# Low parts of split weights by an accumulating DMA instead of a VectorE subtraction

## The chip, the cores and the metric

The kernel runs on one core of a Trainium2 chip. The metric is the device time of one execution in microseconds (us), as the median over runs. The engines are TensorE (PE for its matmuls, PEld for its weight loads), VectorE (DVE), ScalarE (ACT), GpSimd (POOL) and SyncE (SP), which issues all transfers of the kernel before the change.

## The reference

Two layers of a trunk with 512 latent tokens and 256 context tokens, width 1024, in float32. In each layer one wide projection `h @ w_in` (1024 by 7456) feeds three branches: grouped-query attention, a chunked bidirectional gated linear attention (GLA) and a gated mixing MLP (SGU). Each branch is gated and projected, the three are merged under sigmoid gates, projected by `w_out`, and normalised:

```python
h = x * (1 + scale) + shift
parts = split(h @ w_in)
m = sig(m_a) * (y_attn @ w_br_attn) + sig(m_g) * (y_gla @ w_br_gla) + sig(m_s) * (y_sgu @ w_br_sgu)
x_new = layer_norm(ALPHA * x + gate * (m @ w_out))
```

Layer 0 computes all 768 tokens in its output, layer 1 only the 512 latent ones.

## The kernel before

**Split products.** TensorE's fast 32-bit format keeps fewer bits than float32. So each operand of a large product is held as a high part (the value rounded to that format) and a low part (the value minus the high part). A product is three matmuls: high by high, low by high, high by low. `mm3` issues them for one block of 128 rows of the contraction.

**Weights.** `wgroup(src, nkb, c0, n)` brings a group of `nkb` blocks of 128 rows and `n` columns (mostly 8 or 4 blocks of 256 columns) on chip. It works in units of two blocks: a tile `raw` (256 KB) is loaded by a transfer that SP issues; `split(hi, lo, raw)` then lets ACT write `hi` (a copy with rounding, `act`) and DVE or POOL write `lo = raw - hi` (`tta`, line 128 in the trace, where the planner chooses the engine). There are 3 buffers of `raw` and 5 each of `hi` and `lo`, so of a group of four units only one more unit of the next group fits beside it; the others wait until TensorE has read the last use of an old one. With `scale` (only `w_out` of layer 1) `raw` is first multiplied by a gate.

By the code there are 284 units without `scale`: 220 of `w_in`, 48 of the three branch projections, 16 of `w_out` in layer 0. The 12 or so others of `lo`, and the first group of layer 0 (`wl`), go another way.

**Uses.** `cm` makes 128 output columns for the 512 latent tokens and then the 256 context tokens (layer 0) out of one group: one pass over all 8 blocks for each of 2 column blocks and each token set. `tm` makes 128 tokens by 256 columns at a time, one pass for each tile of tokens. Passes accumulate in PSUM buffers of the tag `p`, of which there are two.

**Order.** Nothing is issued in the order of the code. Each operation is recorded with its engine, operands and a cost in ns from `_cost`; `Sched.order` plays the queues of the five engines with these costs, with fixed lags between engines (`LAT`: 280 from ACT to TensorE, 172 from ACT to POOL, 200 where none is listed), and with the buffers; it repeats this 16 times with new priorities and keeps the shortest plan. `issue` then emits that order; each engine runs its queue in order. A choice such as `tta` (DVE or POOL) is made in the plan. A transfer on SP is planned with 1300 ns before and 700 ns after its data.

**Stages by time.** Start and first projections (0 to 72 us); layer 0 with attention, GLA and projections between them (72 to 434); its branch projections, merge and output (434 to 905); the same for layer 1 (905 to 1195, 1195 to 1376, and the end to 1448).

Of the kernel before, what the change touches and what calls it, by code (L numbers as in the profile page):

```python
# [13 lines left out]
ALU = mybir.AluOpType  # L14
AX = mybir.AxisListType
PSUM = bass.MemoryType.PSUM
# [11 lines left out]
class Sched:  # L28
# [8 lines left out]
    def __init__(self, nc):  # L37
        self.nc = nc
        self.ops = []
        self.port = []  # L40
        self.tiles = {}
        self.tags = {}
        self.state = {}
        self.masks = {}
        self.bias = 0.0
        self.floor = -1e9
        self.label = "start"
        for n, e in (("PE", nc.tensor), ("ACT", nc.scalar), ("DVE", nc.vector), ("POOL", nc.gpsimd), ("SP", nc.sync)):
            setattr(self, n, _Eng(self, n, e))
# [88 lines left out]
    def order(self, prio):  # L138
# [4 lines left out]
        n = len(ops)  # L143
# [10 lines left out]
        for o in ops:  # L154
            for x in sorted(o[3]):
                if x not in place:
                    k = self.tiles[x][1]
# [31 lines left out]
        def can(i):  # L189

            need = {}
            for t in missing(i):
                k, idx = place[t]
                need.setdefault(k, []).append(idx)
            for k, l in need.items():
                if sorted(l) != list(range(alloc[k], alloc[k] + len(l))) or live[k] + len(l) > self.tags[k][0]:
                    return k
            return None
# [17 lines left out]
        while done < n:  # L216
            best = None
            for e in engs:
                L, R = later[e], ready[e]
                while L and (L[0][0] <= free[e] or gone[L[0][1]]):  # L220
                    a, i = heapq.heappop(L)
# [12 lines left out]
            t, e = best  # L234
            R, L = ready[e], later[e]
            while L and L[0][0] <= t:
                a, i = heapq.heappop(L)
                if not gone[i]:
                    heapq.heappush(R, (prio[i], i))
            i = None  # L240
# [4 lines left out]
            if e == "ACT" and len(R) > 1:  # L245
                c = min(R, key=lambda x: x[0] + (self.SWITCH if ops[x[1]][5] not in (None, cur) else 0))
                R.remove(c)
                heapq.heapify(R)
                i = c[1]
            elif e == "PE" and len(R) > 1:  # L250
                while recent and recent[0][0] < t - self.TICK:
                    dense -= recent.popleft()[1]
                if dense < self.WARM and ops[R[0][1]][8] < 0.5:
                    c = min(R, key=lambda x: x[0] + (1e6 if ops[x[1]][8] < 0.5 else 0))
                    R.remove(c)
                    heapq.heapify(R)
                    i = c[1]
                else:
                    i = heapq.heappop(R)[1]
            elif e in held and R and held[other[e]] > t + 1.0:  # L260

                w = held[other[e]] - t
                c = min(R, key=lambda x: x[0] + (self.HOLD * w if e in self.port[x[1]] else 0.0))
                R.remove(c)
                heapq.heapify(R)
                i = c[1]
            else:
                i = heapq.heappop(R)[1]
# [11 lines left out]
            k = can(i)  # L280
# [14 lines left out]
            st = t  # L295
            if e in held and e in self.port[i]:
                st = max(st, held[other[e]])
            if e == "ACT" and ops[i][5] not in (None, cur):
                st = max(st, acted + 1283.0)
                cur = ops[i][5]  # L300
            ks = set()
            for x in list(missing(i)):
# [11 lines left out]
                st = max(st, r_)  # L314
# [10 lines left out]
            if e == "SP":  # L325
                dma = max(dma, st + 1300.0) + cost
                free[e] = max(st + 60.0, dma - self.AHEAD)
                end = dma + 700.0
            else:
                end = free[e] = st + cost  # L330
                if e == "ACT":
                    acted = end
                if e in held and e in self.port[i]:
                    held[e] = end
# [32 lines left out]
        for i in reversed(seq):  # L367
            e = gone[i]
# [34 lines left out]
class _Eng:  # L403
# [3 lines left out]
    def __getattr__(self, meth):  # L407
        real = getattr(self.e, meth)
        s, n = self.s, self.n

        def call(*a, **k):
            aps = [x for x in a if isinstance(x, bass.AP)]
            outs, ins = [], []
            if "out" in k:
                outs.append(k["out"])
            else:
                outs.append(aps.pop(0))
            if isinstance(k.get("accum_out"), bass.AP):
                outs.append(k["accum_out"])
            ins = aps + [v for q, v in k.items() if isinstance(v, bass.AP) and q not in ("out", "accum_out")]  # L420
            return s.record(n, lambda: real(*a, **k), outs, ins, _cost(n, meth, outs, ins, k), _table(n, k), _dens(n, ins, k), _port(n, meth, outs, ins))  # L421

        return call


def _dens(n, ins, k):
    if n != "PE":
        return 0.0
    d = ins[0].ap[0][1] / 128.0
    return 0.7 * d if "tile_position" in k else d  # L430


def _port(n, meth, outs, ins):

    inside = [x for x in ins if x.space == bass.MemoryType.SB and any(c > 1 for _, c in x.ap[1:])]
    if n == "POOL":
        return (n,) if any(x.space == bass.MemoryType.SB for x in ins) else ()
    if n == "DVE":
        psum = any(x.space == PSUM for x in list(ins) + list(outs))
        if len(inside) > 1 or meth in ("tensor_copy", "tensor_scalar") and not psum:  # L440
            return (n,)
    return ()


def _table(n, k):
    f = str(k.get("func", "")).split(".")[-1]
    return Sched.TABLE.get(f) if n == "ACT" else None


def _cost(n, meth, outs, ins, k):  # L450
    o = outs[0]
    sz = 1
    for _, c in o.ap[1:]:
        sz *= c
    if n == "PE":
        if meth == "transpose":
            return 62.0 if ins[0].dtype == F32R else 110.0
        m = 1
        for _, c in ins[0].ap[1:]:
            m *= c  # L460
        if ins[0].dtype == F32R:
            return max(0.4475 * sz + 2.5, 0.84 * m)
        if "tile_position" in k:
            return 21.0 + 0.4 * sz
        return max(1.73 * sz, 1.68 * m) + 2
    ptr = sum(isinstance(k.get(q), bass.AP) for q in ("scale", "bias", "scalar", "scalar1", "scalar2"))
    if n == "ACT":
        return 0.8333 * sz + (50 if str(ins[0].space).endswith("PSUM") else 93) + 94.0 * ptr + (93.0 if len(outs) > 1 else 0)
    if n == "DVE":
        psum = any(str(x.space).endswith("PSUM") for x in ins + outs)  # L470
        if meth == "tensor_tensor_scan":
            return 2 * sz / 0.96 + 50
        if len(outs) > 1:
            return (sz + 64) / 0.96 + 40
        if meth == "reciprocal":
            return 8 * sz / 0.96 + 60
        if meth == "tensor_reduce" or meth == "bn_stats":
            sz = 1
            for _, c in ins[0].ap[1:]:
                sz *= c  # L480
        if meth in ("tensor_copy", "tensor_scalar", "memset") and not psum:
            return (sz / 2 + 64) / 0.96 + 62.0 * ptr
        return (sz + 64) / 0.96 + 62.0 * ptr
    if n == "POOL":
        if k.get("op") == ALU.pow:
            return 165.0 * sz + 300
        if meth == "tensor_tensor":
            few = any(st == 0 and c > 1 for x in ins for st, c in x.ap[1:])
            return (1.7 if few else 2.2) * sz + 125
        if meth == "scalar_tensor_tensor":  # L490
            return 1.4 * sz + 95
        if meth == "memset":
            return 0.5 * sz + 50
        return 0.9 * sz + (135 if meth == "tensor_copy" else 175)
    b = 4
    for _, c in o.ap:
        b *= c
    return b / 335.0
# [3 lines left out]
def kernel(ctx: ExitStack, tc: tile.TileContext, A, out, dbg=None):  # L502
    nc = tc.nc
    sc = Sched(nc)
    ACT, DVE, POOL, PE, SP = sc.ACT, sc.DVE, sc.POOL, sc.PE, sc.SP
# [8 lines left out]
    def T(tag, shape, dt=F32, name=None):  # L514
        return sc.tile(sb, shape, dt, tag, BUFS.get(tag, 1), name or tag, "SB")
# [14 lines left out]
    def act(out, in_, func=AF.Copy, **kw):  # L530
        return ACT.activation(out=out, in_=in_, func=func, **kw)
# [12 lines left out]
    def f(ap):  # L544
        return ap.bitcast(F32)
# [20 lines left out]
    def tta(out, in0, in1, op):  # L566
        k = dict(out=out, in0=in0, in1=in1, op=op)
        return sc.alt((DVE, "tensor_tensor", k), (POOL, "tensor_tensor", k))

    def split(hi, lo, src):  # L570
        act(hi, src)
        tta(lo, src, f(hi), ALU.subtract)
# [20 lines left out]
    CUT, LAST = 608, 832  # L593
    FILL, GPROJ, EV = 8000.0, 4000.0, 20000.0
    WB = 20000.0

    def wgroup(src, nkb, c0, n, tags=None, scale=None):

        tiles = []
        if tags:  # L600
            wide = [T(t, [128, nkb, n], F32R, name="wide") for t in tags]
        for q in range(nkb // 2):
            if True:
                sc.bias -= WB
                raw = T("raw", [128, 2, n])
                SP.dma_start(
                    out=raw, in_=src[q * 256:(q + 1) * 256, c0:c0 + n].rearrange("(k p) n -> p k n", p=128)
                )
                if scale is not None:
                    tta(raw, raw, scale.unsqueeze(1).to_broadcast([128, 2, n]), ALU.mult)  # L610
                if tags:
                    hi, lo = (t[:, 2 * q:2 * q + 2] for t in wide)
                else:
                    hi = T("hi", [128, 2, n], F32R)
                    lo = T("lo", [128, 2, n], F32R)
                split(hi, lo, raw)
                sc.bias += WB
            tiles += [(hi[:, 0], lo[:, 0]), (hi[:, 1], lo[:, 1])]
        return tiles
# [974 lines left out]
```

## Time and profile before

| what | value |
|---|---|
| time, median of 3 runs (lowest, highest) | 1450.51 us (1448.73, 1452.96) |
| profiled execution: time, span from first to last instruction | 1449.78 us, 1448.0 us |
| busy: TensorE, VectorE, ScalarE, GpSimd | 1397.2, 1041.7, 664.4, 140.8 us |
| mean granted clock of TensorE | 0.994 of full speed |
| read from HBM, written | 134.76 MB, 14.69 MB |

The 1.8 us between the profiled execution's time and its span lie around the instructions. Busy times are unions of intervals on one engine; a matmul's end is modelled, so the rate of TensorE is read from the starts of consecutive matmuls.

### The profile page before, as it was taken

The numbers are of one execution on the slowest core, as the hardware profiler recorded it, in microseconds if no ns is written. First come the engines' busy times: TensorE is split into PE (matmuls) and PEld (weight loads), VectorE is DVE, ScalarE is ACT, GpSimd is POOL, SyncE is SP. The second block draws the span as 40 slices with busy tenths as digits, with TensorE's granted clock in tenths as the row PEclk, the third lists the DMA queues.
The fourth block names the chain that finished last, engine by engine and source line by source line (L and its number), as shares of the span: only waits on it lengthen the run. The fifth ranks groups of instructions, "written<-read, shape, count | busy, mean of one in ns | idle before, by whom it ended". The sixth has DMA issues, their size and how long they took to land. (4 is left out here: it accounts for less than half of the span.)

```text
span 1448.0 us, 27281 instructions
## 1 busy us (share of the span) xinstructions
PE 1397.2 (96%) x10724; PEld 1232.3 (85%) x10724; DVE 1041.7 (72%) x2252; ACT 664.4 (46%) x1275; POOL 140.8 (10%) x223
## 2 busy tenths in 40 slices
PE   8899999999999999999999999999999879999997
PEld 5798989888888888888889999888977668888887
DVE  8968887998968778422176776898898975433397
ACT  4557666845452224212231365667755443432331
POOL 0031110033310000000000011100023200000003
PEclk9999999999999999999999999999999999999999
DMA  9410002322284554212232332012433265334342
GB/s 323 159 32 19 21 27 65 123 85 71 61 267 152 158 178 143 79 50 73 59 117 88 103 104 62 8 30 74 123 109 91 74 218 175 95 102 109 95 160 95
DMA packets 115890, 151.23 MB, mean 104 GB/s; under 512 B 8601, under 2 KB 89905, under 8 KB 115761
## 3 DMA queue, kind: packets, MB, share of 16 engines
q1 hardware_dynamic: 115762, 149.49, 33.8%
q8 instruction: 84, 1.38, 0.4%
q14 instruction: 44, 0.36, 0.1%
HBM read 134.76 MB, written 14.69 MB: 103 GB/s over the span
## 5 line engine op out<-in xcount | busy, mean ns | idle before, releaser
L128 DVE TENSOR_TENSOR lo<-raw,hi 128x512 fp32r<-128x512 f32 (+1 forms) x295 | 202.9, 695 | 215.5 <-ACT hi L421 206.5
L421 PE MATMUL p<-hlh,hi 128*128 128x512 f32 x704 | 281.6, 400 | 6.1 <-ACT sg L421 3.9
L421 ACT ACTIVATE hi<-raw 128x512 fp32r<-128x512 f32 (+1 forms) x296 | 185.2, 633 | 220.0 <-PE p L421 145.4
L421 PE MATMUL p<-hll,hi 128*128 128x512 f32 x704 | 280.8, 399 | 0.0
L421 PE MATMUL p<-hlh,lo 128*128 128x512 f32 x704 | 280.5, 399 | 0.0
L421 PEld LDWEIGHTS p<-hlh,hi 128*128 128x128 f32 x704 | 132.7, 188 | 34.0 <-ACT sg L421 4.1
L421 PEld LDWEIGHTS p<-hlh,lo 128*128 128x128 f32 x704 | 132.9, 189 | 30.1 <-DVE lo L128 1.1
L421 PEld LDWEIGHTS p<-hll,hi 128*128 128x128 f32 x704 | 132.6, 188 | 26.2
L421 PE MATMUL p<-hch,lo 128*128 128x256 f32 x368 | 104.3, 283 | 0.0
L421 PE MATMUL p<-hcl,hi 128*128 128x256 f32 x368 | 104.3, 283 | 0.0
L421 PE MATMUL p<-hch,hi 128*128 128x256 f32 x368 | 104.2, 283 | 0.0
L421 PE MATMUL p<-hi,hlh 128*128 128x256 f32 (+1 forms) x352 | 101.7, 289 | 0.0
L421 PE MATMUL p<-hi,hll 128*128 128x256 f32 (+1 forms) x352 | 100.5, 286 | 0.0
L421 PE MATMUL p<-lo,hlh 128*128 128x256 f32 (+1 forms) x352 | 99.9, 284 | 0.0
L421 ACT ACTIVATE sig<-p 128x512 f32<-128x512 f32 (+1 forms) x48 | 25.3, 527 | 129.7 <-PE p L421 128.8
L421 POOL TENSOR_SCALAR sf<-sf 128x1 f32<-128x1 f32 x20 | 10.1, 505 | 687.5 <-DVE sf L421 687.0
L421 ACT ACTIVATE P<-s,sm 128x768 f32<-128x768 f32 (+1 forms) x80 | 65.3, 820 | 23.5 <-DVE sm L421 22.9
L421 DVE TENSOR_REDUCE sm<-s 128x1 f32<-128x768 f32 (+1 forms) x72 | 64.8, 921 | 9.6 <-PE s L421 9.5
L421 DVE TENSOR_TENSOR PTs<-pt,PTs 128x512 fp32r<-128x512 f32 x104 | 69.5, 684 | 2.7 <-ACT PTs L421 2.0
L421 PEld LDWEIGHTS p<-hch,hi 128*128 128x128 f32 x368 | 69.5, 189 | 2.0
L421 DVE SCALAR_TENSOR_TENSOR wada<-wada,srow 128x512 f32<-128x512 f32 x96 | 65.5, 689 | 7.7 <-DMA wada<-in_w_adaT_dram 6.3
L421 PEld LDWEIGHTS p<-hcl,hi 128*128 128x128 f32 x368 | 69.3, 188 | 2.1
(296 smaller groups left out, 3386.5 us busy)
## 6 DMA issues: line engine op xcount, KB each, us to landing
raw<-in_w_in_dram SPq DMA_DIRECT2D x204, 256.0 KB, 2.9
wada<-in_w_adaT_dram SPq DMA_DIRECT2D x80, 256.0 KB, 4.5
raw<-in_w_out_dram SPq DMA_DIRECT2D x32, 256.0 KB, 2.9
raw<-in_w_in_dram SPq DMA_DIRECT2D x16, 272.0 KB, 2.9
wada<-in_w_adaT_dram SPq DMA_DIRECT2D x8, 512.0 KB, 5.5
raw<-in_w_br_attn_dram SPq DMA_DIRECT2D x16, 256.0 KB, 3.6
raw<-in_w_br_gla_dram SPq DMA_DIRECT2D x16, 256.0 KB, 3.0
raw<-in_w_br_sgu_dram SPq DMA_DIRECT2D x16, 256.0 KB, 3.0
```

The lines of the kernel that those rows point to most:

```text
L128: fns[p.n] = lambda real=real, k=k: real(**k)
L421: return s.record(n, lambda: real(*a, **k), outs, ins, _cost(n, meth, outs, ins, k), _table(n, k), _dens(n, ins, k), _port(n, meth, outs, ...
```

## The change

In `wgroup`, for every unit without `scale`, the subtraction goes. ACT writes `hi` as before and then writes minus the high part into `lo` (the same copy with scale -1). A transfer issued by GpSimd then reads the same weights from DRAM a second time and adds them to `lo` in place. The planner gets a cost of 1000 ns for this issue on POOL and 2500 ns more until its result is there. Also some planner figures change: 125 ns more for ACT and DVE operations of fewer than 128 partitions, less for DVE operations with a second output (40 to 12), 125 ns for `bn_aggr`.

```diff
@@ order
                 end = free[e] = st + cost
+                if e == "POOL" and i in self.swdge:
+                    end += 2500.0
@@ _cost
+    few = 125.0 if o.ap[0][1] < 128 and n != "POOL" else 0.0
     if n == "ACT":
-        return 0.8333 * sz + ...
+        return few + 0.8333 * sz + ...
     if n == "DVE":
         if len(outs) > 1:
-            return (sz + 64) / 0.96 + 40
+            return (sz + 64) / 0.96 + 12
+        if meth == "bn_aggr":
+            return 125.0
...
-        return (sz + 64) / 0.96 + 62.0 * ptr
+        return few + (sz + 64) / 0.96 + 62.0 * ptr
     if n == "POOL":
+        if meth == "dma_start":
+            return 1000.0
@@ wgroup
-                split(hi, lo, raw)
+                if DMALO and scale is None:
+                    act(hi, raw)
+                    act(lo, raw, scale=-1.0)
+                    POOL.dma_start(out=lo, in_=src[q * 256:(q + 1) * 256, c0:c0 + n].rearrange("(k p) n -> p k n", p=128), accum_op=ALU.add)
+                else:
+                    split(hi, lo, raw)
```

`DMALO` is true; the rest of the diff notes which POOL operations are such transfers and renames a variable.

## Rows read from the trace of the kernel before

**Rows 1.** The page's busy line: us, share of the span, instructions.
```profile
PE 1397.2 (96%) x10724; PEld 1232.3 (85%) x10724; DVE 1041.7 (72%) x2252; ACT 664.4 (46%) x1275; POOL 140.8 (10%) x223
```
**Rows 2.** Windows by stage: length, busy us of each engine, clock, DMA share, GB/s.
```profile
0.00:72.00 72.00, 62.59 (x295) 47.78 (x296) 64.49 (x204) 36.50 (x69) 2.00 (x10) 1.00 0.70 242
72.00:290.00 218.00, 214.40 (x1578) 199.62 (x1577) 182.73 (x379) 150.26 (x321) 28.75 (x36) 1.00 0.17 48
290.00:434.00 144.00, 137.96 (x2079) 118.95 (x2078) 123.55 (x261) 70.92 (x122) 40.99 (x63) 1.00 0.39 121
434.00:905.00 471.00, 470.43 (x3093) 428.95 (x3093) 281.26 (x624) 154.51 (x306) 16.12 (x24) 1.00 0.34 105
905.00:1050.00 145.00, 142.26 (x1007) 130.41 (x1006) 123.48 (x247) 103.14 (x198) 6.85 (x11) 1.00 0.21 59
1050.00:1158.00 108.00, 98.25 (x1292) 78.33 (x1292) 99.06 (x255) 53.80 (x105) 31.49 (x62) 0.98 0.33 92
1158.00:1195.00 37.00, 28.96 (x171) 23.71 (x170) 26.97 (x47) 18.19 (x31) 1.20 (x2) 0.94 0.67 213
1195.00:1376.00 181.00, 181.00 (x779) 146.65 (x778) 78.68 (x135) 59.77 (x101) 0.00 (x0) 0.99 0.41 115
1376.00:1448.00 72.00, 61.39 (x444) 57.90 (x442) 61.45 (x108) 17.33 (x27) 13.44 (x16) 0.94 0.37 128
```
**Rows 3.** Waits of TensorE, 1050 to 1158, then 1158 to 1195: us, times, longest.
```profile
PE s L119 <- DVE M L128: 4.2, 3, 1.7
PE s L119 <- DVE Ac L421: 1.7, 3, 0.8
...
PE pt L421 <- DVE sv L128: 4.2, 1, 4.2
```
**Rows 4.** Windows of DVE's instructions on `lo` alone, same stages.
```profile
290.00:434.00 144.00, 16.35 (x24) 1.00 0.39 121
434.00:905.00 471.00, 76.67 (x112) 1.00 0.34 105
...
1050.00:1158.00 108.00, 18.23 (x25) 0.98 0.33 92
...
1195.00:1376.00 181.00, 45.59 (x66) 0.99 0.41 115
```
**Rows 5.** Groups by shape: the subtraction on DVE, the copy on ACT.
```profile
L128 DVE TENSOR_TENSOR lo<-raw,hi 128x512 fp32r<-128x512 f32 x279 | 191.6, 693 | 201.8 <-ACT hi L421 194.9 <-PE p L421 4.7 <-issue 0.5
...
L421 ACT ACTIVATE hi<-raw 128x512 fp32r<-128x512 f32 x280 | 174.9, 632 | 211.5 <-PE p L421 143.7 <-DMA raw<-in_w_in_dram 28.6 <-DVE lo L128 17.3
```
**Rows 6.** Timeline of ACT, then of TensorE, between two groups of layer 0.
```profile
676.98 2.06 ACT L421 ACTIVATE hi<-raw 128x512 fp32r<-128x512 f32 x3
...
676.19 0.28 PE L421 MATMUL p<-hch,hi 128*128 128x256 f32 x1
676.31 0.28 PE L421 MATMUL p<-hcl,hi 128*128 128x256 f32 x1
...
679.05 0.40 PE L421 MATMUL p<-hlh,hi 128*128 128x512 f32 x1
...
680.90 0.40 PE L421 MATMUL p<-hlh,lo 128*128 128x512 f32 x1
```
**Rows 7.** The same between two groups of layer 1.
```profile
1329.89 0.63 ACT L421 ACTIVATE hi<-raw 128x512 fp32r<-128x512 f32 x1 [0.57 <-PE p L421]
...
1335.94 0.39 PE L421 MATMUL p<-hlh,lo 128*128 128x512 f32 x1
```
**Rows 8.** DMA issues of the page: count, KB each, median us to landing.
```profile
raw<-in_w_in_dram SPq DMA_DIRECT2D x204, 256.0 KB, 2.9
wada<-in_w_adaT_dram SPq DMA_DIRECT2D x80, 256.0 KB, 4.5
...
wada<-in_w_adaT_dram SPq DMA_DIRECT2D x8, 512.0 KB, 5.5
```

More of the change, by code (lines that the diff above doesn't have):

```diff
@@ L40, in __init__ @@
         self.port = []
+        self.swdge = set()
         self.tiles = {}
@@ L420, in call @@
             ins = aps + [v for q, v in k.items() if isinstance(v, bass.AP) and q not in ("out", "accum_out")]
+            if n == "POOL" and meth == "dma_start":
+                s.swdge.add(len(s.ops))
             return s.record(n, lambda: real(*a, **k), outs, ins, _cost(n, meth, outs, ins, k), _table(n, k), _dens(n, ins, k), _port(n, meth, outs, ins))
@@ L465, in _cost @@
         return max(1.73 * sz, 1.68 * m) + 2
+    few = 125.0 if o.ap[0][1] < 128 and n != "POOL" else 0.0
     ptr = sum(isinstance(k.get(q), bass.AP) for q in ("scale", "bias", "scalar", "scalar1", "scalar2"))
     if n == "ACT":
-        return 0.8333 * sz + (50 if str(ins[0].space).endswith("PSUM") else 93) + 94.0 * ptr + (93.0 if len(outs) > 1 else 0)
+        return few + 0.8333 * sz + (50 if str(ins[0].space).endswith("PSUM") else 93) + 94.0 * ptr + (93.0 if len(outs) > 1 else 0)
     if n == "DVE":
@@ L481, in _cost @@
         if meth in ("tensor_copy", "tensor_scalar", "memset") and not psum:
-            return (sz / 2 + 64) / 0.96 + 62.0 * ptr
-        return (sz + 64) / 0.96 + 62.0 * ptr
+            return few + (sz / 2 + 64) / 0.96 + 62.0 * ptr
+        return few + (sz + 64) / 0.96 + 62.0 * ptr
     if n == "POOL":
+        if meth == "dma_start":
+            return 1000.0
         if k.get("op") == ALU.pow:
@@ L487, in _cost @@
         if meth == "tensor_tensor":
-            few = any(st == 0 and c > 1 for x in ins for st, c in x.ap[1:])
-            return (1.7 if few else 2.2) * sz + 125
+            rep = any(st == 0 and c > 1 for x in ins for st, c in x.ap[1:])
+            return (1.7 if rep else 2.2) * sz + 125
         if meth == "scalar_tensor_tensor":
@@ L595 @@
     WB = 20000.0
+    DMALO = True
     def wgroup(src, nkb, c0, n, tags=None, scale=None):
```

## The prediction

> **What bounds the kernel now.** I read the busy line first. TensorE is busy for 1397.2 us of a span of 1448.0 us [rows 1]. The most that better feeding could give is therefore the 50.8 us in which it is idle; everything else has to be looked at as a risk to that busy time.
>
> The second view is the windows by stage, read as length minus TensorE's busy time [rows 2]. The start (0 to 72) has 9.4 us idle, 72 to 290 has 3.6, 290 to 434 has 6.0, 434 to 905 only 0.6, 905 to 1050 has 2.7, 1050 to 1158 has 9.8, 1158 to 1195 has 8.0, 1195 to 1376 none, and the end 10.6. So the kernel consists of two sorts of stages. In the long projection stages (652 us together) TensorE never waits. In the mixed stages VectorE is nearly as full as TensorE: 99.1 of 108 us at 1050 to 1158, where it is the busier of the two, and 123.6 of 144 at 290 to 434 [rows 2]. The waits of TensorE confirm it for the first of these: the longest are on VectorE's products for GLA (4.2 us on `M`, 1.7 on `Ac`), and in the next stage one of 4.2 us on `sv` [rows 3].
>
> The third view is VectorE's work on `lo` alone, by the same stages: 18.2 of its 99.1 us at 1050 to 1158, 16.4 of its 123.6 at 290 to 434, but most of it (76.7 and 45.6 us) in the two long stages where VectorE is not short of time [rows 4].
>
> **The change part by part.**
>
> *Removed.* 284 subtractions by 0.693 us, nearly all on VectorE: 197 us of its 1041.7 [rows 1, 5]. In the long stages this is worth nothing, as TensorE is the bound there. In the mixed stages I count a share of the idle time. At 1050 to 1158 VectorE falls from 99.1 to 80.8 us beside 98.3 of TensorE, which then becomes the bound; I take 6 of the 9.8 us, about what its named waits on VectorE add up to [rows 2 to 4]. At 290 to 434 VectorE falls to 107.2; half of 6.0 is 3. At 72 to 290 and 905 to 1050 there are 6.3 us idle together, of which I take 2. At 1158 to 1195 I take 2 of 8.0, since what comes before `sv` there includes transfers that stay. Sum: 13 us gained. The bounds are 0 (the chains of GLA stay as long as they are, with work for one engine less in parallel) and 30 (all idle time of these five stages). Start and end hold no or few of these subtractions and stay.
>
> *Added on ScalarE.* 284 copies by 0.632 us, 179 us [rows 5]; its total becomes 844 us. The fullest stage is 905 to 1050: 103.1 us plus 20 units by 0.632 is 115.8 of 145. At 1050 to 1158 it is 53.8 plus 15.8, or 70 of 108 [rows 2, 4]. Idle time hides it. Where it does not, in the queue between two units, it is counted next.
>
> *Added in the chain of a unit.* This is where the change can cost. A unit's buffers become free when TensorE has read the old unit for the last time, and its `lo` must be ready when TensorE comes to it. In layer 0, between two groups, the trace shows the copy into the freed `hi` starting at 676.98, the new group's first matmul at 679.05, and the matmul that reads the `lo` of that unit, the ninth of the pass, at 680.90: a lead of 3.92 us [rows 6]. Before, copy and subtraction need 0.63 + 0.69 us and a hand-over, so some 2 us are left over. In layer 1, where a pass has 512 columns throughout, the same lead is 1335.94 - 1329.89 = 6.05 us [rows 7].
>
> After the change the chain is the copy of minus high (0.63), the hand-over to POOL (0.17, the planner's lag), the transfer from its issue to its landing, and the hand-over to TensorE (0.2). If ACT writes `hi` first it is 0.63 longer. The price of the transfer is not in the trace. From below: a load of the same 256 KB by SP lands 2.9 us after its issue. From above: 512 KB, which is what a transfer that reads both the weights and `lo` moves in, took 5.5 us beside other traffic [rows 8]. I take 3.9: the 2.9 of the like load, plus the 1.0 by which 512 KB took longer than 256 KB of the same tensor. It is nearer to the lower end because the weight loads are the nearest row in pattern and stage.
>
> The chain is then 0.63 + 0.17 + 3.9 + 0.2 = 4.9 us with `lo` written first, 5.5 with `hi` first. Against the lead of 3.92 us in layer 0 that is 1.0 or 1.6 us late. Some of it is filled: the first unit of the new group is there, and TensorE has the pass over the context tokens for it (6 matmuls of 0.12 us by the spacing of their starts, 0.7 us [rows 6]), in the second PSUM buffer. What is left is 0.3 or 0.9 us. As the planner orders by due time, and is told 3.5 us for the transfer, it will mostly place `lo` first; I take 0.4. In 434 to 905 I count 16 places of this kind: 8 pairs of an eight-block and a four-block group, 4 groups of the third gate, 4 of the output. 16 by 0.4 is 6.4 us. In the mixed stages attention and GLA fill most of it; I add 0.6. In layer 1 the chain (4.9 to 5.5) fits into 6.05 us: nothing. Sum: 7 us lost. Its bounds: with the 2.9 us of the plain load nothing is lost (chain 3.9); with 5.5 us it is (6.5 - 3.92 - 0.7) = 1.9 by 16, or 30 us, plus about 10 in the mixed stages and 0.5 by 12 groups in layer 1: 46 us.
>
> A rule of the Trainium skill gives another price. Its page "DMA: Bandwidth & Descriptors", section "Anatomy of one DMA — SWDGE (gpsimd) path", fits a GpSimd-issued transfer as about 2.0 us plus bytes over 436 GB/s. For 256 KB that is an estimate of 2.6 us, and by it the chain would keep within the lead and the sum would be 13 us gained; no run here shows such a transfer yet, and even the plain loads took 2.9 [rows 8].
>
> *Added on GpSimd.* 284 issues in a queue that is busy for 140.8 us [rows 1]. Queued behind an issue that waits for ACT stand the small powers of the norms and some of GLA's `M`. GpSimd is mostly idle, and stays so even at 1 us an issue; if that cover is gone, a norm comes 1 us late, and attention or GLA behind it. I count nothing.
>
> *Added on the DMA engines.* 74 MB more to read from DRAM. The free SP queue is not touched. In 1195 to 1376 the share is 0.41 at 115 GB/s [rows 2]; 66 units [rows 4] bring 17.3 MB beside the 20.8 there (115 GB/s by 181 us), so at the price of a plain load 0.41 by 17.3 / 20.8 = 0.34 more, 0.75 in all. That is hidden; at double price it is not (third rival).
>
> *Refitted figures.* They change no operation, only the order. Either sign is possible; 3 us either way, taken as 0.
>
> **Sum.** 1449.8 - 13 + 7 = 1443.8 against the profiled execution's own time; the median is 0.7 us above that, so 1444.5; I say 1444.
>
> **The rivals.**
>
> *The transfer lands late (slower).* If issue to landing takes 5.0 us, `lo` is 6.0 - 3.92 - 0.7 = 1.4 us late at each of the 16 places, 22 us, and about 0.5 at 20 more in the mixed stages, 10 us. With 13 gained: 1449.8 + 19 = 1469. It decides from a price of about 4.3 us, where 16 by 0.8 eats the 13 us. For it: 256 KB of `wada` took 4.5 us [rows 8], and the branch stage of layer 0 loads that tensor too. Against it: the median load of `w_in` lands in 2.9.
>
> *VectorE is not what the mixed stages wait for (no change).* The 13 us shrink to some 7, because GLA's chain alternates between ACT, DVE and TensorE and its length stays; the 7 lost eat the rest: 1450. For it: of the idle time at 1158 to 1195 only half is named as VectorE [rows 2, 3].
>
> *The DMA engines fill up (slower).* If an added 256 KB costs them twice a load, 1195 to 1376 needs 0.41 + 0.69 = 1.10 of their time, 199 us for 181, or 18 us more; with 13 gained and 7 lost 1462. The skill's page "Collectives: The Full Stack", section "The bandwidth ceiling: the fold count and why AG ≠ RS ≠ AR", says that an addition in a transfer needs two source reads and so runs at half the rate, which is this mechanism; no row here shows an adding transfer.
>
> **How the numbers follow.** The forecast's case has 0.40, and from 1434 to 1447 its own range. No change has 0.20, the late landing 0.30, the full DMA engines 0.10. What a measurement of this kernel can tell from no change is about 0.3%, 4.4 us. A few of the slower cases end inside that band and some of the no-change case ends faster: faster 0.42, within 0.20, slower 0.38. The range for 8 in 10 takes in the late landing at its 5 us and leaves out the 5.5 us end and the best 30 us gained: 1432 to 1472.
>
> **What would show it.** Right: VectorE's busy time falls to about 845 us and ScalarE's rises to about 844; idle time of TensorE at 1050 to 1158 falls by some 6 us; in the layer 0 projections short waits on the transfer into `lo` appear, 0.3 to 0.5 us each, and none in layer 1; issue to landing near 3.9 us. Wrong: waits of TensorE on that transfer of a microsecond and more in many groups, or a DMA share near 0.9 in layer 1's projections, or a mixed stage that is no shorter although VectorE has time.

## The result, and the profile after

The changed kernel takes 1729.43 us (median of 4 runs, 1723.86 to 1731.08) against 1451.74 of the kernel before (4 runs, 1448.73 to 1454.36): a ratio of 1.1909, 95% interval 1.1893 to 1.1925. It is slower by 278 us, where 1444 us and at most 1472 were forecast. The profiled execution took 1731.08 us, 1729.2 of them span; its mean granted clock is 0.947, where it was 0.994.

The page after: the busy line, the two DMA queues with data (packets, MB, share of 16 engines), and the median us from issue to landing for the weight loads and the additions.

```profile
PE 1490.8 (86%) x10724; PEld 1287.6 (74%) x10724; DVE 864.7 (50%) x1966; ACT 798.4 (46%) x1557; POOL 486.2 (28%) x507
...
q0 software_dynamic: 77248, 74.73, 29.3%
q1 hardware_dynamic: 115762, 149.49, 28.5%
...
raw<-in_w_in_dram SPq DMA_DIRECT2D x204, 256.0 KB, 4.8
lo<-in_w_in_dram POOLq DMA_DIRECT2D x204, 256.0 KB, 7.4
```

Against [rows 1] the work moved as it was meant to: VectorE fell by 177 us, ScalarE rose by 134. But TensorE, with the same 10724 matmuls, is busy for 93.6 us more, and it is idle for 238.4 us (1729.2 - 1490.8) instead of 50.8, which is 187.6 more. The two make the 281 us by which the span grew. An addition lands 7.4 us after its issue, and the plain loads beside it land in 4.8, where they took 2.9 [rows 8].

To see where this lies, both traces are cut at the same four events: the first mixing matmul of the gated MLP in layer 0, the last multiplication of layer 0's output by its gate, the last mixing matmul in layer 1, and the first multiplication of `w_out` by its gate. The columns are those of [rows 2]. Before:

```profile
0.00:433.80 433.80, 414.76 (x3947) 366.14 (x3948) 370.57 (x842) 257.69 (x510) 71.73 (x108) 1.00 0.33 104
433.80:834.70 400.90, 400.39 (x2509) 359.54 (x2510) 234.84 (x526) 112.04 (x206) 6.39 (x10) 1.00 0.36 110
834.70:1189.10 354.40, 337.69 (x3044) 300.55 (x3043) 290.26 (x635) 215.30 (x429) 49.27 (x89) 0.99 0.31 90
1189.10:1376.50 187.40, 183.52 (x789) 148.57 (x788) 85.05 (x146) 62.07 (x103) 0.00 (x0) 0.99 0.40 112
1376.50:1448.00 71.50, 60.89 (x442) 57.48 (x440) 60.95 (x108) 17.33 (x27) 13.44 (x16) 0.94 0.37 127
```

After:

```profile
0.00:496.40 496.40, 438.20 (x3996) 383.22 (x3997) 341.33 (x794) 292.63 (x578) 140.02 (x166) 0.97 0.50 128
496.40:1027.70 531.30, 443.45 (x2451) 387.39 (x2452) 173.48 (x419) 146.42 (x289) 112.69 (x98) 0.90 0.56 120
1027.70:1421.30 393.60, 349.30 (x3027) 307.49 (x3027) 248.41 (x571) 244.31 (x493) 137.96 (x161) 0.95 0.59 126
1421.30:1657.80 236.50, 200.72 (x820) 154.53 (x819) 41.65 (x80) 98.01 (x173) 80.97 (x68) 0.98 0.84 168
1657.80:1729.20 71.40, 59.08 (x437) 54.94 (x435) 59.85 (x105) 16.97 (x28) 14.61 (x17) 0.97 0.41 134
```

The lengths differ by 62.6, 130.4, 39.2, 49.1 and -0.1 us. The orders differ, so a stretch does not hold quite the same matmuls (2451 against 2509 in the second). The last stage, in which only the last of the new transfers is issued, is untouched. The second and the fourth, in which TensorE had hardly waited, lost 179.5 of the 281.2 us. In the fourth the DMA share is 0.84, about twice what it was.

The waits of TensorE after (us in total, times, longest):

```profile
PE p L426 <- DMA lo<-in_w_in_dram: 138.8, 86, 7.5
PE p L426 <- DMA lo<-in_w_br_attn_dram: 22.3, 8, 4.0
PE p L426 <- DMA lo<-in_w_br_gla_dram: 18.7, 8, 3.4
PE p L426 <- DMA lo<-in_w_out_dram: 13.9, 6, 3.8
...
PE p L426 <- DMA lo<-in_w_br_sgu_dram: 3.6, 2, 2.5
```

They name the cause of most of the 238.4 us of idle time: 197.3 us in 110 waits, all on the new transfer. No other wait in the list exceeds 6.1 us. One group of the third gate in layer 0 shows how they come about, in the timeline of ScalarE, then GpSimd, then TensorE:

```profile
824.15 0.63 ACT L426 ACTIVATE hi<-raw 128x512 fp32r<-128x512 f32 x1
824.69 1.66 ACT L426 ACTIVATE lo<-raw 128x512 fp32r<-128x512 f32 x3
...
825.60 4.92 POOL L426 DMA_DIRECT2D lo<-in_w_in_dram  x4 [18.64 <-ACT lo L426]
848.04 4.91 POOL L426 DMA_DIRECT2D lo<-in_w_in_dram  x4 [17.52 <-ACT lo L426]
...
832.29 0.50 PE L426 MATMUL p<-hlh,lo 128*128 128x512 f32 x1 [3.17 <-DMA lo<-in_w_in_dram]
...
834.47 0.51 PE L426 MATMUL p<-hlh,lo 128*128 128x512 f32 x1 [0.51 <-DMA lo<-in_w_in_dram]
...
836.59 0.51 PE L426 MATMUL p<-hlh,lo 128*128 128x512 f32 x1 [0.45 <-DMA lo<-in_w_in_dram]
```

ScalarE writes minus the high part of three units ahead of most of the `hi`, as forecast, and TensorE passes its time with the other token set. But the four additions are issued together, from 825.60 on. TensorE gets the first of the awaited units 6.7 us later (832.29 - 825.60), and the next two 2.2 and 2.1 us after that. A unit of a 512-column pass is 6 matmuls of 0.23 us, 1.4 us, so TensorE outruns the landings and waits again for each. From one set of issues to the next it is 22.4 us, while the group's matmuls, 48 of 0.23 and 48 of 0.12 us, fill 16.9. Such sets are common: counting issues less than 2.5 us apart as one set, 128 of the 284 additions come in sets of four and 120 in sets of two or three, and within a set the landings lie 2.2 us apart (median).

The DMA queues in 825 to 838, with what was issued there:

```profile
q0 software_dynamic: 1088, 1.05, 58.1%
q1 hardware_dynamic: 1088, 1.05, 29.6%
...
raw<-in_w_in_dram SPq DMA_DIRECT2D x4, 256.0 KB, 5.5
lo<-in_w_in_dram POOLq DMA_DIRECT2D x4, 256.0 KB, 8.5
```

Four loads and four additions of the same size share the DMA engines here. The additions take 58.1% of 13 us, 1.9 us each of all 16 engines; the loads 29.6%, 0.96 us each. So a group of four units needs 11.4 us of the DMA engines. In layer 1, where its matmuls need 48 by 0.23 = 11.2 us, that is all the time there is.

What TensorE does after such a wait shows in windows of 2 us behind the next set (same columns; the clock is the third number from the end), and in two of its matmuls there:

```profile
852.00:854.00 2.00, 0.51 (x2) 0.47 (x3) 0.00 (x0) 0.00 (x0) 0.95 (x1) 1.00 1.14 244
854.00:856.00 2.00, 1.28 (x5) 0.58 (x4) 0.00 (x0) 0.00 (x0) 0.00 (x0) 0.71 1.18 237
856.00:858.00 2.00, 1.45 (x4) 1.16 (x4) 0.00 (x0) 0.00 (x0) 0.00 (x0) 0.50 1.22 202
858.00:860.00 2.00, 2.00 (x6) 1.61 (x5) 0.00 (x0) 0.00 (x0) 0.00 (x0) 0.50 0.35 55
860.00:862.00 2.00, 2.00 (x9) 1.71 (x9) 0.00 (x0) 0.60 (x1) 0.00 (x0) 0.58 0.00 0
862.00:864.00 2.00, 2.00 (x16) 1.87 (x15) 0.00 (x0) 0.39 (x1) 0.00 (x0) 1.00 0.00 0
```

```profile
858.43 0.63 PE L426 MATMUL p<-hlh,hi 128*128 128x512 f32 x1
858.85 0.63 PE L426 MATMUL p<-hll,hi 128*128 128x512 f32 x1
```

TensorE is busy for 1.8 of the 4 us from 852 to 856. In the second half of them the granted clock falls from 1.00 to 0.50, the lower of its two levels (1.2 GHz). It rises again between 860 and 862, at about 861.7 by that window's 0.58, though TensorE has had no gap since 856.55 (the 1.45 us of that window and all of the next two): for some 5 us it is full and slow. Matmuls of 512 columns start 0.42 us apart there (858.43 and 858.85), where it is 0.23 at the higher level. Not every wait is followed by this: behind the 3.17 us before 832.29 the clock stays at 1.00. Over the second stage the clock is 0.90, and 0.10 of its 443 us is 44 us, about what the stage's busy time grew by (43.1). So a wait can be paid twice: once as idle time, once as slow matmuls behind it. DMA shares just above 1 are read as full.

### The profile page after: what moved, and what is told of

Its sections match the earlier page's. It is cut to its first block, busy times and chain, and to the rows that moved or that the text cites. A ratio compares the mean times of both kernels' runs of the same rounds, so it can differ in the third digit from the quotient of the medians.

```text
span 1729.2 us, 27819 instructions
## 1 busy us (share of the span) xinstructions
PE 1490.8 (86%) x10724; PEld 1287.6 (74%) x10724; DVE 864.7 (50%) x1966; ACT 798.4 (46%) x1557; POOL 486.2 (28%) x507
## 3 DMA queue, kind: packets, MB, share of 16 engines
q0 software_dynamic: 77248, 74.73, 29.3%
## 4 chain that ended last, share of the span: by engine, by line
issue 39%; PE 26%; DMA 14%; POOL 12%; DVE 6%; ACT 2%; SPq 0%; POOLq 0%; ACTq 0%; DVEq 0%
PE p L426 18%; DMA lo<-in_w_in_dram 12%; POOL lo L426 10%; PE pt L426 4%; PE s L426 3%; DVE sm L426 1%; PE s L120 1%; DVE junk L426 1%; DVE wada L426 1%; POOL sm L426 1%; DMA kept<-agd 1%; POOL M L129 1%; DMA lo<-in_w_out_dram 0%; POOL sg L426 0%; DVE wl L129 0%
## 5 line engine op out<-in xcount | busy, mean ns | idle before, releaser
L426 POOL DMA_DIRECT2D lo<-in_w_in_dram x220 | 273.4, 1385 | 597.0 <-ACT lo L426 519.8
L426 PE MATMUL p<-hlh,lo 128*128 128x512 f32 x704 | 295.7, 421 | 105.1 <-DMA lo<-in_w_in_dram 104.7
L426 PE MATMUL p<-hlh,hi 128*128 128x512 f32 x704 | 287.1, 408 | 1.4 <-ACT sg L426 0.7
L426 ACT ACTIVATE lo<-raw 128x512 fp32r<-128x512 f32 (+1 forms) x284 | 173.0, 623 | 70.5 <-PE p L426 53.7
L426 PE MATMUL p<-lo,hlh 128*128 128x256 f32 (+1 forms) x352 | 108.8, 309 | 34.2 <-DMA lo<-in_w_in_dram 34.1
L426 PE MATMUL p<-yh,lo 128*128 128x512 f32 (+1 forms) x192 | 74.9, 398 | 41.0 <-DMA lo<-in_w_br_attn_dram 22.3
L426 PEld LDWEIGHTS p<-lo,hlh 128*128 128x128 f32 x352 | 71.9, 204 | 39.3 <-DMA lo<-in_w_in_dram 39.2
L426 DVE TENSOR_TENSOR sig<-p,sig 128x512 f32<-128x512 f32 (+1 forms) x24 | 14.5, 603 | 169.9 <-PE p L426 168.4
L426 DVE TENSOR_TENSOR sgS<-p,sgS 128x512 f32<-128x512 f32 (+1 forms) x24 | 14.3, 598 | 163.7 <-PE p L426 163.7
L426 PE MATMUL p<-lo,mlh 128*128 128x256 f32 x224 | 68.2, 305 | 14.3 <-DMA lo<-in_w_out_dram 13.9
```

## The experiments

**The parts of the change.** Three kernels take it apart: one without the transfer, one with the refitted figures alone, and one with neither, in which only the work moves.

```diff
 no_transfer:
-  POOL.dma_start(out=lo, in_=src[...], accum_op=ALU.add)
 refit_only:
-  DMALO = True
+  DMALO = False
 no_transfer_old_figures: as no_transfer, and
-  few = 125.0 if o.ap[0][1] < 128 and n != "POOL" else 0.0
+  few = 0.0
-  return (sz + 64) / 0.96 + 12
-  if meth == "bn_aggr": return 125.0
+  return (sz + 64) / 0.96 + 40
```

> ScalarE still writes minus the high part, but no transfer adds the weights: the low part stays minus the high part, planned anew without it. All of the loss then goes if it comes from the transfer, and what is left is the gain of taking the subtractions off VectorE. By the prediction's term of 13 us the time is 1435 to 1442; if VectorE is not what the mixed stages wait for, 1446 to 1454; if ScalarE's 179 us more are what costs, above 1480.

> The weights are split as before; only the planner's refitted figures are in. If the transfer is the cause, 1447 to 1455 (the prediction's 3 us either way). If the new order made by the refitted figures carries a part of the loss, more than 1460.

> As the run without any transfer (the low part stays minus the high part), with the planner's narrow figures as before the change. The relief of VectorE alone, in the order made by the old figures: by the prediction's term 1437 to 1442; by the run with the new figures, 3.7 us below the kernel before, 1443 to 1449.

| kernel | time, us | ratio to before (95%) |
|---|---|---|
| no_transfer | 1447.59 (11 runs) | 0.9972 (0.9961 to 0.9984) |
| refit_only | 1453.84 (11 runs) | 1.0024 (1.0011 to 1.0037) |
| no_transfer_old_figures | 1438.44 (5 runs) | 0.9904 (0.9889 to 0.9920) |

Relief of VectorE alone is worth 13.3 us (1451.74 - 1438.44). The refit alone costs 2.6 us against the 1451.28 of that chip, and 9.2 together with the moved work (1447.59 - 1438.44, on two chips, each beside the same kernel before). The rest, 1729.43 - 1447.59 = 281.8 us, comes with the transfer. no_transfer by itself fell into the range that its expectation gave to VectorE not being what the mixed stages wait for; the relief shows only in the order made by the old figures. Three windows of no_transfer_old_figures:

```profile
290.00:434.00 144.00, 136.42 (x2072) 117.29 (x2071) 115.84 (x251) 86.43 (x154) 39.72 (x60) 0.99 0.38 120
...
1050.00:1158.00 108.00, 100.87 (x1348) 79.80 (x1347) 91.86 (x248) 73.41 (x141) 31.66 (x63) 1.00 0.38 112
1158.00:1195.00 37.00, 36.61 (x176) 30.11 (x175) 24.56 (x47) 25.25 (x45) 0.00 (x0) 1.00 0.76 242
```

In the last two TensorE is idle for 7.1 and 0.4 us, where it was 9.8 and 8.0 [rows 2]. As all later work begins earlier, the two are read together: 10.3 us less, in the mixed stages in which VectorE was short. At 290 to 434 the relief shows nothing: TensorE is idle for 7.6 us, where it was 6.0.

**What of the transfer costs: a copy in its place, and half of it.**

```diff
 copy_not_add:
-  POOL.dma_start(out=lo, in_=src[...], accum_op=ALU.add)
+  POOL.dma_start(out=lo, in_=src[...])
 half_added:
-  POOL.dma_start(out=lo, in_=src[...], accum_op=ALU.add)
+  POOL.dma_start(out=lo[:, 0], in_=src[q * 256:q * 256 + 128, c0:c0 + n], accum_op=ALU.add)
```

> The same plan and order, but GpSimd's transfer copies the weights over the low part instead of adding to it, so the low part is wrong and one read of the destination is left out. If the addition is what makes the transfer slow (its queue took 29.3% of the DMA engines for 74.7 MB, against 28.5% for 149.5 MB of plain transfers), issue to landing falls from 7.4 to about 4.5 us, the queue's share to about 15%, TensorE's waits on it from about 200 to under 60 us, and the time to 1500 to 1560. If it is the way through GpSimd and not the addition, landing stays at 6.5 us or more and the time above 1680.

> The change with the same plan, but each transfer adds only the first of the unit's two blocks (128 KB; the low part of the second block stays minus its high part). If bytes through the DMA engines make the price, issue to landing falls from 7.4 to 4.5 to 5.5 us and the time to 1520 to 1600. If it is a fixed latency of an adding transfer, landing stays above 6.3 and the time above 1660.

The copy gives 1528.61 us and the half addition 1522.17 (one run each). The page of copy_not_add: the queue and the landing.

```profile
q0 software_dynamic: 77248, 74.73, 20.4%
...
lo<-in_w_in_dram POOLq DMA_DIRECT2D x204, 256.0 KB, 5.0
```

The same bytes, written and not added, take 20.4% of 1526.8 us, 311 us of all DMA engines, against 29.3% of 1729.2, 507 us. They land in 5.0 us instead of 7.4; landing and time are near the first forecast, the queue's share is above its 15%. Of the 281.8 us, 81.0 are there with a plain copy, and the other 200.8 come with the adding. Half the bytes added land in 4.9 us and cost 74.6 us, a quarter of the whole, so the loss grows faster than the size.

**The price by itself.** Two kernels do none of the reference's work: single transfers and sets of four, each with nothing beside it (prices), and sets of four additions alone and beside four loads (crowd).

```diff
+ nc.sync.dma_start(out=spload, in_=w)
+ nc.gpsimd.dma_start(out=copyr, in_=w)
+ nc.gpsimd.dma_start(out=addr, in_=w, accum_op=ALU.add)
+ # the same for 128 and 512 KB; four at once; four beside four loads
```

> No part of the reference is computed, the output is zero: single transfers with nothing beside them, each awaited before the next (256 KB in rows of 1 KB by SyncE, by GpSimd as a copy with and without conversion, by GpSimd as an addition; additions of 128 and 512 KB), then four at once of each kind. If the addition is dear in itself, one of 256 KB takes 4.5 us or more alone, at least 1 us more than GpSimd's copy, its price grows by 1.5 us or more per further 256 KB, and four at once land at twice the spacing of four copies. If it is the crowding in the kernel that makes 7.4 us, one alone takes 3.5 us, as the planner was told, and the addition costs little over the copy.

> No part of the reference is computed, the output is zero: four additions of 256 KB issued by GpSimd one behind the other, alone, then with four loads of 256 KB by SyncE at the same time, then one addition with one load. If crowding makes 7.4 us out of the 4.5 of an addition alone, the four take 4.4 to 7.5 alone, as measured, and a median of 7 or more beside the loads, and one beside one load 5 to 6. If they stay as alone, the rest comes from something else in the kernel.

Median us from issue to landing in prices (the two kernels took 296.27 and 198.77 us, which says nothing by itself):

```profile
adddouble<-in_w_in_dram POOLq DMA_DIRECT2D x6, 512.0 KB, 6.2
...
spload<-in_w_in_dram SPq DMA_DIRECT2D x6, 256.0 KB, 2.7
...
copyr<-in_w_in_dram POOLq DMA_DIRECT2D x6, 256.0 KB, 3.1
...
addr<-in_w_in_dram POOLq DMA_DIRECT2D x6, 256.0 KB, 4.5
...
fourcopyd<-in_w_in_dram POOLq DMA_DIRECT2D x4, 256.0 KB, 4.0
...
fouraddd<-in_w_in_dram POOLq DMA_DIRECT2D x4, 256.0 KB, 7.5
addhalf<-in_w_in_dram POOLq DMA_DIRECT2D x6, 128.0 KB, 3.1
```

In crowd, where a line mixes sets alone with sets beside loads:

```profile
fouraddd<-in_w_in_dram POOLq DMA_DIRECT2D x12, 256.0 KB, 9.4
...
fourloadd<-in_w_in_dram SPq DMA_DIRECT2D x6, 256.0 KB, 6.5
```

A lone addition lands in 4.5 us, 1.4 more than the copy. Of four at once the last takes 7.5, and the last of four copies 4.0. In these sets GpSimd issues the additions 0.7 to 0.9 us apart, and they land 1.6 to 2.1 us apart (mean of each set); four copies, issued 0.7 us apart, land 0.9 to 1.0 apart. So each addition holds back the next, by about the 1.9 us for which it kept the DMA engines above. Beside four loads the last addition takes 9.4 to 9.9 us (10.8 in a set that a store of 512 KB overlapped; the line's 9.4 is the median over both kinds of set), and the last load 6.5, where four loads alone took 4.2. By order of issue the medians in crowd are 4.6, 5.8, 7.0 and 7.6 us alone and 6.9, 8.4, 9.0 and 9.6 beside four loads; in the kernel they are 6.2, 7.4, 8.9 and 8.7. So the kernel's median of 7.4 us is what additions in sets beside loads take, with no other cause needed. One addition beside one load takes 4.9, a little under the 5 to 6 expected.

**Would a better plan hide it?** plan_told gives the planner a price near the measured one; six_buffers adds a sixth buffer of `hi` and `lo`, so that two units of the next group fit ahead and not one.

```diff
 plan_told:
-  end += 2500.0
+  end += 6000.0
-  return 1000.0
+  return 1250.0
 six_buffers: as plan_told, and
-  "hi": 5, "lo": 5, "S3": 8
+  "hi": 6, "lo": 6, "S3": 7
```

> The change with the planner told what the trace shows: 1250 ns for the issue on GpSimd and 6000 ns more until the result, in place of 1000 and 2500. If most of the loss is that the order was made for a price that is half the real one, the time falls to 1480 to 1600. If five buffers leave no order in which TensorE does not wait, it stays above 1650.

> As the run with the planner told the price, with six buffers of high and low parts instead of five (and seven instead of eight of the 3 KB working tiles, to make room). If the lead that the buffers leave is what TensorE waits for, a unit more of it (4.2 us in layer 0, 2.8 in layer 1) takes the time from 1657 to 1500 to 1580. If the DMA engines' throughput bounds it, it stays above 1630.

They take 1657.13 and 1540.69 us (one run each): the first is above the 1650 of its second forecast, the second inside the 1500 to 1580 of its first. The first wait on `lo` of each, plan_told and then six_buffers, and for six_buffers the window between the last mixing matmul in layer 1 and the first multiplication of `w_out` by its gate:

```profile
PE p L426 <- DMA lo<-in_w_in_dram: 52.3, 49, 2.9
```

```profile
PE p L426 <- DMA lo<-in_w_in_dram: 20.3, 19, 3.4
```

```profile
1261.20:1461.60 200.40, 197.99 (x846) 157.07 (x844) 38.80 (x75) 100.30 (x177) 84.21 (x70) 1.00 0.98 200
```

With the price known 72.3 us come back, with one more buffer another 116.4. The additions of `w_in` still land in 7.7 us with six buffers, so it is the lead that changed, not the transfer. In layer 1's long stage, the fourth of the cut above, TensorE is then idle for 2.4 of 200.4 us, and the DMA engines are at 0.98: it was the lead that was missing there, and with the lead the engines are all but used up. Still 90 us are lost against before (1450.21 on that chip).

**Where it would be free.** layer1_only keeps the transfer to layer 1's branches and gates, where nothing was forecast to be lost; fill_only keeps it to the projections between attention and GLA, where VectorE had been short of time, with the price told and the old figures.

```diff
 layer1_only:
-  if DMALO and scale is None:
+  if sc.label in ("1brA", "1brG", "1ms", "1brS") and scale is None:
 fill_only: end += 6000.0, POOL cost 1250.0, old figures, and
-  if DMALO and scale is None:
+  if sc.label[1:] == "fill" and scale is None:
```

> The change with the figures as made, but the transfer only in the branch, gate and merge stages of layer 1, where the prediction found a lead of 6.05 us and counted nothing lost. With the landing of about 7.2 us that the changed kernel showed there, each of some 12 groups comes 2 us or more late: TensorE's waits on the transfer 20 to 50 us, time 1470 to 1520. If the prediction's step holds once the rest of the kernel is left alone, waits below 8 us and 1447 to 1460.

> The transfer only in the 64 units of the groups that the code files as fill (the kept gates and the SGU input, which may be placed anywhere before their use), with the price told to the planner (1250 and 6000 ns) and none of the other refitted figures. If the loss comes from units that TensorE needs at once, these can wait, and the time is 1440 to 1458, with no wait of TensorE on the transfer beyond 10 us in all. If any such transfer costs its own price, 64 of 220 to 284 give a quarter of the loss, above 1490.

layer1_only takes 1504.54 us (one run), fill_only 1472.9 (4 runs), a ratio of 1.0145 (1.0128 to 1.0161). TensorE's waits on the transfer are 33.4 us in 27 and 11.8 us in 8. The first run is as its first forecast had it; the second lies between its two, above 1458 and below 1490. Windows of layer1_only, then of fill_only:

```profile
1195.00:1435.00 240.00, 203.77 (x832) 156.82 (x831) 48.30 (x93) 98.77 (x173) 80.69 (x67) 0.97 0.82 164
```

```profile
290.00:434.00 144.00, 128.93 (x2007) 110.68 (x2007) 110.24 (x239) 77.35 (x135) 67.56 (x81) 0.98 0.58 145
...
1050.00:1158.00 108.00, 93.95 (x1126) 78.24 (x1125) 85.21 (x227) 72.89 (x136) 53.88 (x76) 0.94 0.74 155
```

In layer 1 TensorE had been busy for all of 181 us [rows 2]; now it is busy for 204 of 240 (832 matmuls instead of 779), with the DMA engines at 0.82, and the kernel is 53 us slower. In the mixed stages VectorE did fall (110.2 and 85.2 us), but TensorE is idle for 15.1 and 14.1 us where it was 6.0 and 9.8 [rows 2]: the DMA share rose from 0.39 to 0.58 and from 0.33 to 0.74, and what the relief gave was more than lost again. How much of that the crowded DMA engines cost, and how much the new order, no run separates. Neither place was free.

**The same addition from the chip's own memory.**

```diff
-  POOL.dma_start(out=lo, in_=src[...], accum_op=ALU.add)
+  POOL.dma_start(out=lo, in_=raw, accum_op=ALU.add)
```

> The change, but the transfer adds the weights from the tile that was just loaded instead of reading DRAM again (planned anew, as that tile is then held longer). If two reads and a write of each row are the price wherever they go, landing stays at 6.5 us or more, the queue's share of the DMA engines at 27% or more, and the time above 1700. If the second read of DRAM is what is slow, landing falls below 5.5 us and the time below 1600.

It takes 1683.85 us (one run), which neither theory expected. The landing falls to 4.1 us and the waits of TensorE on it to 29.4 us. But `raw` has three buffers, and each is now held until the addition has read it: ScalarE waits 205.8 us for loads of `w_in` before it can write `lo`. The stage that loses is another one, and no run shows that this wait is the reason:

```profile
462.00:504.00 42.00, 21.05 (x635) 18.95 (x636) 31.27 (x67) 16.34 (x24) 15.80 (x22) 0.58 0.25 78
```

Half of this window, in the mixed stage, TensorE is idle, at a clock of 0.58. The run also has rows of 2 KB in place of 1 KB (40896 packets on that queue instead of 77248), so whether the read from DRAM or the reading of `lo` makes an addition dear stays open. It does not rest on DRAM alone: the queue still takes 26.7% of 1682.1 us, 449 us.

## Why the prediction was wrong

**What bounds the kernel, and the gain.** The bound was right: TensorE had little to win. The first term's 13 us measured 13.3, in part by luck. In the profiled executions, whose spans differ by 11.3 us, 7.4 us are idle time of TensorE (50.8 to 43.4) and 3.9 are busy time, beside a higher clock (0.997), which the term did not have. For 1050 to 1195, 8 us were taken and 10.3 measured; the 3 us taken at 290 to 434 did not come, as idle time rose there by 1.6.

**The engines.** VectorE has 864.7 us (845 forecast) and ScalarE 798.4 (844): operations in a row overlap at their ends, three copies in 1.66 us, which the forecast's 0.63 and 0.69 each did not have. Summed one by one, VectorE's operations fell by 202 us and ScalarE's rose by 171. That ScalarE could take them free holds in no_transfer_old_figures, where they are all there and the kernel is faster. GpSimd's issues last 1.2 us and not 1.0, though within a set the next begins after some 0.7; no run separates what that alone costs.

**The price of the transfer: the step that failed.** The bounds of 2.9 to 5.5 us hold for one addition alone, which takes 4.5. The forecast added such a lone transfer to each unit's chain. In the kernel most units come in sets of two to four, beside loads, and each addition occupies all DMA engines for 1.9 us: the median is 7.4, and the later ones of a set take up to 11.8. The nearest rows, single loads, could show how long a transfer takes but not how long it keeps the engines from the next.

**The number of places.** It followed from the same mistake. 16 waits of 0.4 us at the joints between groups were forecast, and there are 110 of 1.8 us on average, as the units of a set land some 2.2 us apart and TensorE uses one up in 1.4. With 7.4 us put into the forecast's own sum, 16 places would be (8.4 - 3.92 - 0.7) = 3.8 us late each, 60 us: the count matters as much as the price.

**"In layer 1: nothing."** Wrong, and shown by layer1_only. The third rival had the mechanism and even the amount: it put 199 us of DMA time into that stage, and 0.84 by 236.5 is 199. It priced the stage at the engines' own time, 18 us more, but they are not fed without gaps and the stage grew by 49.1 us; only in six_buffers, with more lead, is it close to that price (200.4 us at 0.98). The Trainium skill's page "Collectives: The Full Stack", section "The bandwidth ceiling: the fold count and why AG ≠ RS ≠ AR", has the addition of a ReduceScatter read two sources and run at half the rate of a copy. The trace agrees against plain loads, with 58.1% and 29.6% of the same window for equal bytes; against GpSimd's own copy the factor is 1.6 (507 and 311 us). That the second read is the reason, no run shows. The Trainium skill's page "DMA: Bandwidth & Descriptors", section "Anatomy of one DMA — SWDGE (gpsimd) path", gave an estimate of 2.6 us for 256 KB; the plain copy took 3.1 alone and the addition 4.5, and the measurement decides.

**The clock.** Not in the forecast at all. TensorE's busy time grew by 93.6 us, a third of the loss, for the same matmuls. By the clock of the five windows, (1 - clock) by busy time is 13 + 44 + 17 + 4 + 2 = 80 us; before, by the same sum, it was 3 + 2 + 4 = 9. So about 71 of the 93.6 us are slow matmuls as in the windows at 852 to 864, and the rest is not shown to be the clock. A part of it can be the breaks themselves: behind a wait in the set at 832 the next matmul starts 0.34 us later and not 0.23, and the last one before it counts with 0.28 us and not with the 0.12 of its spacing. An estimate from these is 0.27 us for each of 110 waits, 30 us. No experiment held the clock fixed.

**The refit.** Taken as 0 within 3 us; it costs 2.6 alone, and about 9 with the relieved VectorE.

**The sum as measured.** 1451.7 - 13.3 (relief) + 9.2 (refit) + 81.0 (transfer as a copy) + 200.8 (adding) = 1729.4. The terms of the last two depend on each other and on the plan, since with six buffers and the price told 188.7 us of them go away.

## What to carry to other kernels

A transfer that hides behind the compute has two prices, its own time from issue to landing and the time for which it keeps the DMA engines; look at how many are issued together and beside which loads, and put the second price into the sum for the whole set. Work taken from an engine that is not the bound is worth at most the idle time of the one that is, here 51 us, and what its gaps cost in clock, so a new dependency in front of the bounding engine, 284 times, has to be shown harmless before anything else. And a wait on TensorE can cost more than its length, because the matmuls behind it can run at the lower clock.

## What was not expected of the hardware

- An adding transfer of 128, 256 and 512 KB lands after 3.1, 4.5 and 6.2 us alone, and its issue is on record on GpSimd for 0.89 to 1.28 us (256 KB: 1.21, against 0.73 for a copy). In a set of four the next issue begins 0.7 to 0.9 us after the one before, but the landings are 1.6 to 2.1 us apart.
- Loads suffer with it: four loads' last landed after 6.5 us beside four additions, 4.2 alone; the kernel's own weight loads went from 2.9 to 4.8 us.
- The granted clock can be watched going from 1.00 to 0.50 and back within 10 us around two waits (852 to 862); for the last 5 us before it rose TensorE had no gap and was still at the lower level.
